# Matmul operands of 16 to 48 rows zero-filled to 128 rows, and two logit matmuls made one, in a hybrid decoder trunk

## The chip, the cores and the metric

The kernel runs on one core of one Trainium2 chip. The metric is the device time of one execution, in microseconds (us), as the median of several runs; lower is better. The engines are named as the profile names them: PE (TensorE, matmuls), PEld (its weight loads), DVE (VectorE), ACT (ScalarE), POOL (GpSimd), SP (SyncE, which only issues DMAs). A DMA that an engine issues is shown with a q behind the engine's name (ACTq).

## What is computed

One layer of a decoder trunk over 16 meta tokens and 512 tokens, model width 2048, all in float32. One input projection feeds three token mixers, and one output projection follows with a residual add and a final norm. Cut to the lines that matter here:

```python
N_META, CHUNK, BLOCK = 16, 64, 128
proj = rms_norm(x, norm_w) @ w_in              # one product for all mixers
(dq, dk, dv, dz, db, da, gq, gk, gv, gz, gl, fq, fk, fv, fz, ff) = split_cols(proj)

# A) gated DeltaNet, 6 heads x 128, chunks of 64
log_a = -exp(a_log) * softplus(da + dt_bias)   # a gate per head and token
g = cumsum(log_a)                              # per chunk
o_dn = gated_delta_rule_chunked(q_dn, k_dn, v_dn, log_a, sigmoid(db))

# B) GLA, 5 heads, key width 64, value width 128, chunks of 64
log_g = log_sigmoid(gl @ w_gk2 + b_gk) / 16    # gl: 16 columns (low rank), w_gk2: 16 x 320
o_gla = gla_chunked(gq, gk, gv, log_g)         # S_t = diag(exp log_g) S_{t-1} + k_t v_t^T

# C) forgetting attention, 5 heads x 128, blocks of 128 queries
c = cumsum(log_sigmoid(ff + b_f))
logits = q_i @ k.T + c_i[:, None] - c[None, :] # masked causally, softmax, times v

o = concat([o_dn, o_gla, o_fox])               # each normed and gated
out = rms_norm(x + o @ w_out)[:, 16:]          # meta tokens are dropped
```

The 16 meta tokens come first in the sequence, so each mixer has, beside four blocks of 128 tokens, a short block of 16.

## The kernel before

**Products and tiles.** Float32 operands of the projections are split into a high and a low part (fp32r), and a product is three matmuls: high by high, high by low, low by high (`inproj_part`, L245; `inproj_pair` and its `product`, L580, for the later columns; `mms`, L1410, for the output projection). A half of an input projection has 1024 weight columns per partition, loaded by `load_half`; `split` casts them on ACT (`whi`, L170) and subtracts on DVE (`wlo`, L171). It is 48 matmuls: 8 slices of the model width, three products, two parts of 264 tokens. Two halves are in flight. These projection matmuls fill PE; the mixers' small matmuls stand between them. A plain float32 matmul (not split) shows in the profile as two passes, a transpose as one.

**Order.** The kernel is written with a tile framework whose scheduler simulates a timeline and from it sets the order of every engine's instructions. A few places are tied by hand: `behind`, `later` and `place` pin a mixer's matmul behind a certain projection matmul, and `split` has priority. Any change to a cost or a dependence can therefore move instructions on all engines. On the chip each engine runs its list in order and waits at semaphores. A DMA is issued from an engine's list too, and a DMA that must wait for data holds up everything behind it on that engine.

**Pools.** Buffers are rings: `six` (14 large tiles: the gates' `gw` and `gcn`, attention operands), `t15` (6 tiles of 128 x 3 x 128: `dg`, `kdm`, `um`, `vpm`, `ym`, `gvm`, `gkm`), `row` (7), and in PSUM `psb` (4 banks, projections) and `psm` (4 banks, all the mixers' results).

**Places that the change touches**, in the order of time:

- *rstd diagonal* (L355 to L360). A matmul of `ones` with a diagonal matrix `dg` broadcasts the reciprocal norms along partitions, per block of 128 tokens; for the meta block (b = 4) both operands have 16 rows.
- *Gates* (`gates`, L456 to L474, and the lines ahead of it). `misc` holds the raw gate columns. `gw` has three rows of 528: `scm`, `gt` and `ga`, of which 17 partitions (32 to 48) are used; `ga` receives the running sum (`tensor_tensor_scan`, L466 on DVE). The sum is written to DRAM (`gd`, issued from ACT), read back as `gb`, spread over 128 partitions, and also transposed on PE (`ptg`, five transposes of 17 rows) into `gcol`. `gcn` (48 rows) holds the GLA low-rank gate `glr` and its weight `wgk`.
- *DeltaNet group g = 0, 1* (three heads each): `dn_keys` forms decays from `gb` and `gcol` (`at`, `e`) and the decayed meta keys `kdm`; `dn_inverse` gives `um`, 16 x 16 used; `dn_values` gives `vpm`; `dn_mix` multiplies `um` by `vpm` (`pym`, L853), copies that to `ym`, and forms the state after the meta tokens from `kdm` and `ym` (`ps0`, L858). All these operands have 16 rows.
- *GLA pair p = 0, 1, 2* (`gla_pair`; pair 2 has one head): `pgk` (L1001) is the low-rank gate, two matmuls of 48 rows; `gvm` and `gkm` are the meta values and keys, 16 rows, multiplied in `pg` (L1103; called pg0 here).
- *Forgetting attention* (`fox_head`): for each of four query blocks b, `pfa` (L1237) is the logits against all keys ahead of the block (16 + 128 b columns) and `pfd` (L1238) those against the block's own 128 keys, in two PSUM tiles.

Of the kernel before, what the change touches and what calls it, by code (L numbers as in the profile page):

```python
# [8 lines left out]
F32 = mybir.dt.float32  # L9
F32R = mybir.dt.float32r  # L10
# [4 lines left out]
ALU = mybir.AluOpType  # L15
# [3 lines left out]
P = 128  # L19
D = 2048  # L20
KT = D // P
NM = 16
S = 512
T = NM + S
HT = T // 2
NB = S // P
EPS = 1e-6
H = 3
# [54 lines left out]
def tile_hybrid_trunk(ctx, tc, xT, xtok, mtok, w_gate, w_in, w_out, w_dn, consts, lmask, fin_w, out, dbg=None):  # L83
# [271 lines left out]
    for b in range(5):  # L355
        r = NM if b == 4 else P
        dg = t15(f"dg{b}", (P, P))
        V.tensor_scalar_mul(dg[:r, :r], ident[:r, :r], rsc[:r, b : b + 1])
        o = pr[1][:, :NM] if b == 4 else pr[0][:, b * P : (b + 1) * P]
        PE.matmul(o, ones[:r], dg[:r, :r], start=True, stop=True)  # L360
    A.copy(rstd[:, NM:], pr[0])
# [85 lines left out]
    V.scalar_tensor_tensor(out=wgk, in0=whi.bitcast(F32), scalar=mcc[:48, 7:8], in1=raw, op0=ALU.mult, op1=ALU.add)  # L447
    A.copy(glr[0:32], misc[0:32])
# [7 lines left out]
    def gates():  # L456
        esc = cst.tile([P, 1], F32, name="esc")
        A.activation(esc[gr], mcc[gr, 2:3], AF.Exp)
        V.tensor_scalar(gt[gr], misc[gr], mcc[gr, 0:1], mcc[gr, 1:2], ALU.add, ALU.mult)
        V.scalar_tensor_tensor(out=ga[gr], in0=gt[gr], scalar=-1.0, in1=gt[gr], op0=ALU.mult, op1=ALU.min)  # L460
        A.activation(ga[gr], ga[gr], AF.Exp)
# [4 lines left out]
        V.tensor_tensor_scan(ga[gr], scm[gr], gt[gr], 0.0, ALU.mult, ALU.add)  # L466
        nc.scalar.dma_start(out=gd[:16], in_=ga[R0 : R0 + 16])
        nc.scalar.dma_start(out=gd[16:], in_=ga[R0 + 16 : R1])
        pt = psm.tile([P, 512], F32, tag="m", name="ptg")
        for b in range(NB):  # L470
            PE.transpose(pt[:, b * 17 : b * 17 + 17], ga[gr, NM + b * P : NM + (b + 1) * P], ident[gr, gr])
        PE.transpose(pt[:NM, 4 * 17 : 5 * 17], ga[gr, 0:NM], ident[gr, gr])
        V.tensor_copy(gcol[:, 0:4, :], pt[:, : 4 * 17].rearrange("p (b r) -> p b r", b=4))
        V.tensor_copy(gcol[:NM, 4, :], pt[:NM, 4 * 17 : 5 * 17])  # L474

# [160 lines left out]
    raw = {}  # L636
# [18 lines left out]
    def dn_keys(g):  # L655
# [25 lines left out]
        for b in (4, 0, 1, 2, 3):  # L681
# [16 lines left out]
            for j in range(H):  # L698
                dst = kd[:, b * H + j, :] if b < 4 else kdm[:, j, :]
                V.tensor_scalar_mul(dst, pk[:r, j * P : (j + 1) * P], e[:r, j, r - 1 : r])  # L700
# [34 lines left out]
    def dn_inverse(g, st):  # L735
# [31 lines left out]
        nc.scalar.dma_start(out=xm, in_=sc3.rearrange("h (a c) -> a h c", a=32))  # L767
        um = t15(f"um{g}", (32, H, 32))
        for o, x in ((um.rearrange("p h c -> p (h c)"), xm.rearrange("p h c -> p (h c)")),
                     (uc.rearrange("p n c -> p (n c)"), xc.rearrange("p n c -> p (n c)"))):  # L770
            waits.append((V.transpose(o, x).ins, len(splits) + SP[g], splits))
# [51 lines left out]
    def dn_values(g, st):  # L823
        vp = six.tile([P, NN, P], F32, tag="six", name=f"vp{g}")
        vpm = t15(f"vpm{g}", (NM, H, P))
        br = st["br"]
        for j in range(H):
            h = H * g + j
            v = row(f"v{h}")[:, :T]
            conv_silu(("dv", h), 12 + h, v)  # L830
            pv = psm.tile([P, 512], F32, tag="m", name=f"pv{h}")
            for b in range(NB):
                PE.transpose(pv[:, b * P : (b + 1) * P], v[:, bsl(b)], ident)
            for b in range(NB):
# [3 lines left out]
            V.tensor_scalar_mul(vpm[:, j, :], pv2[:NM, :P], br[:NM, 4, j : j + 1])  # L838
        st.update(vp=vp, vpm=vpm)
# [7 lines left out]
    def dn_mix(g, st):  # L847
# [4 lines left out]
        for j in range(H):  # L852
            PE.matmul(py[:NM, j * P : (j + 1) * P], st["um"][:NM, j, :NM], st["vpm"][:, j, :], start=True, stop=True)  # L853
        ym = t15(f"ym{g}")
        A.copy(ym[:NM], py[:NM, : H * P].rearrange("p (h d) -> p h d", h=H))
        p0 = psm.tile([P, 512], F32, tag="m", name=f"ps0{g}")
        for j in range(H):
            PE.matmul(p0[:, j * P : (j + 1) * P], st["kdm"][:, j, :], ym[:NM, j, :], start=True, stop=True)  # L858
        sst = t15(f"s0{g}")
# [115 lines left out]
    def gla_pair(p):  # L975
# [17 lines left out]
        x_sums(XSUM.get(p, ()))  # L993
        vm = t15(f"gvm{p}", (NM, 2, P))
        for e in range(ne):
            tok_values(inproj(("gv", 2 * p + e)), f"g{2 * p + e}", (vt3, qk)[e][:, 2], vt[:, e], vm[:, e])

        u, t = vt3[:R, 2], trow[:R, :T]
        for a in range(2):
            pg = psm.tile([P, 512], F32, tag="m", name=f"pgk{p}{a}")  # L1000
            PE.matmul(pg[:R, :HT], wgk[:, P * p : P * p + R], glr[:, a * HT : (a + 1) * HT],  # L1001
                      start=True, stop=True)
            V.tensor_scalar_add(u[:, a * HT : (a + 1) * HT], pg[:R, :HT], bgk[:R, p : p + 1])
# [164 lines left out]
    def fox_head(h):  # L1168
# [63 lines left out]
        for b in range(NB):  # L1232
            m = NM + b * P
            ts = bsl(b)
            pa = psm.tile([P, 512], F32, tag="m", name=f"pfa{h}{b}")
            pd = psm.tile([P, 512], F32, tag="m", name=f"pfd{h}{b}")
            PE.matmul(pa[:, :m], qT[:, ts], kT[:, :m], start=True, stop=True)  # L1237
            PE.matmul(pd[:, :P], qT[:, ts], kT[:, ts], start=True, stop=True)  # L1238
            pr = row(f"fp{h}{b}")[:, :T]
# [446 lines left out]
```

## Time and profile before

| | |
|---|---|
| time, median of 3 runs | 986.06 us (985.29 to 986.82) |
| span of the profiled execution | 986.9 us |
| PE busy | 974.9 us (99%), 7762 matmul passes |
| PEld busy | 893.7 us (91%) |
| DVE busy | 669.3 us (68%) |
| ACT busy | 480.3 us (49%) |
| POOL busy | 216.6 us (22%), 237 instructions |
| PE's share of the chain that ended last | 94% |
| DMA | 191.83 MB, mean 194 GB/s |

The profile gives no other time for its own execution than the span, which is 0.8 us above the median of the runs. A row of a timeline has the start, the busy length, engine, line, operation, output and inputs, the rows and columns of the array in use (PE), the shape, and how many instructions it stands for; lengths of neighbouring matmuls overlap, so what a matmul costs is read from one start to the next.

### The profile page before, as it was taken

Reading aid. Unit: us, or ns where it says so; the run is one execution under the profiler, and the core shown is the slowest. Engines: PE = TensorE matmul, PEld = TensorE weight load, DVE = VectorE, ACT = ScalarE, POOL = GpSimd, SP = SyncE. Lnnn points to the kernel's source line nnn. Section 1 sums busy time; section 2 is a strip of 40 time slices with the busy share of each in tenths; the row PEclk is TensorE's granted clock in tenths of the full one; section 3 lists DMA queues with packets and bytes.
Section 4 is the critical chain, followed back from the end, with each engine's and each line's share of the span. In section 5 each row is a group of like instructions: output and inputs, shape, how many; then the busy total and the mean of one; then the engine's idle time right before and its main releaser. Section 6 shows DMA issues by size and latency. Waiting matters only on the chain.

```text
span 986.9 us, 19830 instructions
## 1 busy us (share of the span) xinstructions
PE 974.9 (99%) x7762; PEld 893.7 (91%) x7762; DVE 669.3 (68%) x1462; ACT 480.3 (49%) x1051; POOL 216.6 (22%) x237
## 2 busy tenths in 40 slices
PE   9999999999999999999999999999999999999996
PEld 8899999899999888899899888899999998888885
DVE  5457786985657986334685756867767777887664
ACT  7654524344456344234446435655555544544354
POOL 0021322222123334201213121323322220000023
PEclk9999999999999999999999999999999999999999
DMA  9835588897458797644646556678766578456534
GB/s 348 296 122 206 162 237 237 233 260 223 128 164 221 209 255 198 157 107 102 158 134 164 145 143 197 186 208 226 205 198 164 191 238 295 162 193 211 193 128 172
DMA packets 70339, 191.83 MB, mean 194 GB/s; under 512 B 14077, under 2 KB 17325, under 8 KB 69476
## 3 DMA queue, kind: packets, MB, share of 16 engines
q1 hardware_dynamic: 46048, 152.53, 45.3%
q0 software_dynamic: 15104, 31.66, 18.2%
q10 hardware_dynamic: 9092, 6.36, 2.2%
q8 instruction: 61, 1.00, 0.4%
q14 instruction: 34, 0.28, 0.1%
HBM read 179.84 MB, written 60.88 MB: 244 GB/s over the span
## 4 chain that ended last, share of the span: by engine, by line
PE 94%; DMA 2%; DVE 1%; issue 1%; ACT 1%; POOL 0%; ACTq 0%; POOLq 0%; DVEq 0%
PE pp L245 46%; PE pp_a L580 8%; PE pq L1410 6%; PE pp L314 5%; PE pa L1410 3%; PE pt L1410 3%; PE ps L1410 3%; PE pp_b L580 2%; PE pp_d L580 2%; PE pp_c L580 2%; PE pr L1410 1%; PE pss L1059 1%; DMA zd<-gqk 1%; PE pgate L431 1%; PE pfo L1285 1%
## 5 line engine op out<-in xcount | busy, mean ns | idle before, releaser
L245 PE MATMUL pp<-xl,whi 128*128 128x264 f32 (+2 forms) x1120 | 273.7, 306 | 0.0
L245 PE MATMUL pp<-xh,whi 128*128 128x264 f32 (+2 forms) x1120 | 272.7, 306 | 0.0
L245 PE MATMUL pp<-xh,wlo 128*128 128x264 f32 (+2 forms) x1120 | 272.1, 305 | 0.0
L170 ACT CAST whi<-raw 128x1024 fp32r<-128x1024 f32 x131 | 137.3, 1048 | 185.1 <-PE pp L245 121.8
L171 DVE TENSOR_TENSOR wlo<-raw,whi 128x1024 fp32r<-128x1024 f32 x131 | 163.3, 1247 | 68.2 <-ACT whi L170 57.6
L245 PEld LDWEIGHTS pp<-xl,whi 128*128 128x128 f32 x1120 | 182.6, 189 | 9.2 <-issue 0.4
L245 PEld LDWEIGHTS pp<-xh,whi 128*128 128x128 f32 x1120 | 182.2, 188 | 9.3 <-issue 0.2
L245 PEld LDWEIGHTS pp<-xh,wlo 128*128 128x128 f32 x1120 | 182.6, 189 | 8.7 <-issue 0.2
L390 POOL TENSOR_SCALAR stc<-cv 128x528 f32<-128x528 f32 (+1 forms) x18 | 28.1, 1563 | 144.1 <-DVE cv L622 141.3
L622 DVE SCALAR_TENSOR_TENSOR cv<-pb,cpk,cv 128x528 f32<-128x528 f32 (+1 forms) x54 | 41.0, 760 | 0.8
L1439 POOL TENSOR_TENSOR acc<-acc,fw 128x512 f32<-128x512 f32 x4 | 6.1, 1537 | 138.6 <-DVE wll L171 138.6
L171 DVE TENSOR_TENSOR wlos<-raws,whis 128x1024 fp32r<-128x1024 f32 x20 | 24.2, 1221 | 15.0 <-ACT whis L170 15.0
L170 ACT CAST whis<-raws 128x1024 fp32r<-128x1024 f32 x20 | 20.7, 1049 | 27.9 <-PE ps L1410 9.4
L580 PE MATMUL pp_a<-t,whi 128*128 128x264 f32 (+1 forms) x224 | 30.3, 283 | 0.0
L580 PEld LDWEIGHTS pp_a<-t,whi 128*128 128x128 f32 x224 | 28.0, 188 | 0.4
L580 PE MATMUL pp_a<-xh,whi 128*128 128x264 f32 x112 | 28.1, 285 | 0.0
L580 PE MATMUL pp_a<-xl,whi 128*128 128x264 f32 x112 | 27.9, 285 | 0.0
L379 DVE TENSOR_TENSOR pb<-pp,rstd 128x264 f32<-128x264 f32 (+1 forms) x36 | 13.8, 422 | 18.9 <-PE pp L245 18.9
L1410 PE MATMUL pq<-whia,a 128*128 128x512 f32 x80 | 25.4, 393 | 0.0
L1410 PE MATMUL ps<-whis,s 128*128 128x512 f32 x80 | 25.4, 394 | 0.0
L1410 PE MATMUL pq<-whis,s 128*128 128x512 f32 x80 | 25.3, 394 | 0.0
L390 POOL TENSOR_SCALAR stdz<-zdz 128x512 f32<-128x512 f32 x6 | 11.2, 1875 | 63.3 <-DVE zdz L408 62.3
(506 smaller groups left out, 2106.4 us busy)
## 6 DMA issues: line engine op xcount, KB each, us to landing
raw<-in_w_in SPq DMA_DIRECT2D x103, 512.0 KB, 4.1
ti<-in_w_in SPq DMA_DIRECT2D x28, 512.0 KB, 5.3
raw<-ti SPq DMA_DIRECT2D x28, 512.0 KB, 4.3
tw<-in_w_dn SPq DMA_DIRECT2D x20, 512.0 KB, 5.1
raws<-tw SPq DMA_DIRECT2D x15, 512.0 KB, 4.2
ti<-in_w_in POOLq DMA_DIRECT2D x14, 512.0 KB, 6.4
ti<-ti POOLq DMA_DIRECT2D x14, 512.0 KB, 6.7
tw<-in_w_dn POOLq DMA_DIRECT2D x10, 512.0 KB, 7.0
```

The lines of the kernel that those rows point to most:

```text
L170: pace[0] = A.copy(hi, raw).ins
L171: pace[1] = V.tensor_tensor(out=lo, in0=raw, in1=hi.bitcast(F32), op=ALU.subtract).ins
L245: mm = PE.matmul(p_[:, :nt], wt[:, j * m : (j + 1) * m], xx[k][:, t0 : t0 + nt], start=(k == 0 and wt is hi and xx is xh), stop=(k == KT - ...
L314: mm = PE.matmul(ps[:, :S], wt[:, j * P : (j + 1) * P], xx[k][:, NM:T], start=(k == 0 and wt is hi and xx is xh), stop=(k == KT - 1 and wt ...
L379: V.tensor_tensor(out=o, in0=p_[rows], in1=rstd[rows, t0 : t0 + n], op=ALU.mult)
L390: maxes.append(G.tensor_scalar_max(t, src, LOW).ins)
L431: PE.matmul(pgate[a][:, :HT], wg[k // 8][:, k % 8, :], xx[k][:, a * HT : (a + 1) * HT], start=(k == 0 and xx is xh), stop=(k == KT - 1 and ...
L580: m = PE.matmul(p_[:, cols], wt[:, j * P : (j + 1) * P], xx[j][part_][:, cols], start=first and i == 0, stop=i == len(todo) - 1, skip_grou ...
L622: V.scalar_tensor_tensor(out=c, in0=pb[:, t0 + w : w + T], scalar=cwc[:, blk, w : w + 1], in1=c, op0=ALU.mult, op1=ALU.add)
L1059: mm = PE.matmul(ps[o0 : o0 + n, b * n : b * n + n], kx[rr, k0 : k0 + n], qx[rr, q0 : q0 + n], start=True, stop=True)
L1285: PE.matmul(po[:, qs], v_[:, js], p_[:, jb, qs], start=(jb + i == 0), stop=False)
L1410: mm = PE.matmul(p_, o_[:, s], w_, start=(first and n == 0), stop=(last and n == 2), skip_group_check=True)
```

## The change

Operands that had 16, 17 or 48 rows get 128 rows, the added ones zero, and the matmuls then use all 128 rows. The zeros come from POOL: a cast of a zero column over all of `gcn`, memsets of `ga` (ahead of the scan), `kdm`, `um`, `vpm`, `ym`, `gvm` and `gkm`. The rstd diagonal takes all rows of the identity, so it needs no fill. The gate transposes write 128 columns each into two PSUM tiles (`ptg`, `ptgm`), and the copies pick the 17 wanted. `pgk` of pair 2 gets 128 instead of 64 columns, `pym` 32 instead of 16 columns. In the attention, blocks 0 to 2 compute `pfa` and `pfd` as one matmul over 16 + 128 (b + 1) keys into one PSUM tile; block 3, whose 528 columns are more than the tile's 512, stays as it was. The projections are not touched. The core of the diff:

```diff
-        V.tensor_scalar_mul(dg[:r, :r], ident[:r, :r], rsc[:r, b : b + 1])
+        V.tensor_scalar_mul(dg[:, :r], ident[:, :r], rsc[:, b : b + 1])
-        PE.matmul(o, ones[:r], dg[:r, :r], start=True, stop=True)
+        PE.matmul(o, ones, dg[:, :r], start=True, stop=True)
...
-    gcn = six.tile([48, T + 320], F32R, tag="six", name="gcn")
+    gcn = six.tile([P, T + 384], F32R, tag="six", name="gcn")
+    G.tensor_copy(gcn, zero_c.to_broadcast([P, T + 384]))
...
+        G.memset(ga, 0.0)
         V.tensor_tensor_scan(ga[gr], scm[gr], gt[gr], 0.0, ALU.mult, ALU.add)
...
-            PE.transpose(pt[:, b * 17 : b * 17 + 17], ga[gr, NM + b * P : NM + (b + 1) * P], ident[gr, gr])
-        PE.transpose(pt[:NM, 4 * 17 : 5 * 17], ga[gr, 0:NM], ident[gr, gr])
+            PE.transpose(pt[:, b * P : (b + 1) * P], ga[:, NM + b * P : NM + (b + 1) * P], ident)
+        ptm = psm.tile([P, 512], F32, tag="m", name="ptgm")
+        PE.transpose(ptm[:NM, :P], ga[:, 0:NM], ident)
...
-        kdm = t15(f"kdm{g}", (NM, H, P))
+        kdm = t15(f"kdm{g}")
+        G.memset(kdm, 0.0)
...
-        um = t15(f"um{g}", (32, H, 32))
+        um = t15(f"um{g}", (P, H, 32))
+        G.memset(um, 0.0)
...
-        vpm = t15(f"vpm{g}", (NM, H, P))
+        vpm = t15(f"vpm{g}")
+        G.memset(vpm, 0.0)
...
-            PE.matmul(py[:NM, j * P : (j + 1) * P], st["um"][:NM, j, :NM], st["vpm"][:, j, :], start=True, stop=True)
+            PE.matmul(py[:32, j * P : (j + 1) * P], st["um"][:, j, :], st["vpm"][:, j, :], start=True, stop=True)
         ym = t15(f"ym{g}")
+        G.memset(ym, 0.0)
...
-            PE.matmul(p0[:, j * P : (j + 1) * P], st["kdm"][:, j, :], ym[:NM, j, :], start=True, stop=True)
+            PE.matmul(p0[:, j * P : (j + 1) * P], st["kdm"][:, j, :], ym[:, j, :], start=True, stop=True)
...
-        vm = t15(f"gvm{p}", (NM, 2, P))
+        vm = t15(f"gvm{p}", (P, 2, P))
+        G.memset(vm, 0.0)
...
-            PE.matmul(pg[:R, :HT], wgk[:, P * p : P * p + R], glr[:, a * HT : (a + 1) * HT],
+            PE.matmul(pg[:, :HT], wgk[:, P * p : P * p + P], glr[:, a * HT : (a + 1) * HT],
...
-        km = t15(f"gkm{p}", (NM, P))
-        A.copy(km[:, :R], pm[:NM, :R])
+        km = t15(f"gkm{p}", (P, P))
+        G.memset(km, 0.0)
+        A.copy(km[:NM, :R], pm[:NM, :R])
...
-            pd = psm.tile([P, 512], F32, tag="m", name=f"pfd{h}{b}")
-            PE.matmul(pa[:, :m], qT[:, ts], kT[:, :m], start=True, stop=True)
-            PE.matmul(pd[:, :P], qT[:, ts], kT[:, ts], start=True, stop=True)
+            if b < NB - 1:
+                pd = pa[:, m : m + P]
+                PE.matmul(pa[:, : m + P], qT[:, ts], kT[:, : m + P], start=True, stop=True)
+            else:
+                pd = psm.tile([P, 512], F32, tag="m", name=f"pfd{h}{b}")
+                PE.matmul(pa[:, :m], qT[:, ts], kT[:, :m], start=True, stop=True)
+                PE.matmul(pd[:, :P], qT[:, ts], kT[:, ts], start=True, stop=True)
```

**How the order moves.** Because the scheduler works from costs, the change moves instructions. The largest move is on DVE at the gates. Before, from the third gate step (L463) to the split of the next half; L379, L620 and L622 evacuate and convolve a projection result, L466 is the scan, which the listing shows by its general name:

```order
L379 TENSOR_TENSOR pb_687<-pp_0_689,rstd 128x264
L379 TENSOR_TENSOR pb_687<-pp_1_690,rstd 128x264
L620 TENSOR_SCALAR cv_803<-pb_687,cpk 128x528
L171 TENSOR_TENSOR wlo_1_877<-raw_1_873,whi_1_876 128x1024
L622 SCALAR_TENSOR_TENSOR cv_803<-pb_687,cpk,cv_803 128x528
L463 SCALAR_TENSOR_TENSOR gw<-gw 17x528
L622 SCALAR_TENSOR_TENSOR cv_803<-pb_687,cpk,cv_803 128x528
L464 TENSOR_SCALAR gw<-gw,esc,cpk 17x528
L622 SCALAR_TENSOR_TENSOR cv_803<-pb_687,cpk,cv_803 128x528
L466 SCALAR_TENSOR_TENSOR gw<-gw 17x528
L171 TENSOR_TENSOR wlo_0_949<-raw_0_945,whi_0_948 128x1024
```

Now (L464, L465 and L468 are the former L463, L464 and L466):

```order
L464 SCALAR_TENSOR_TENSOR gw<-gw 17x528
L465 TENSOR_SCALAR gw<-gw,esc,cpk 17x528
L468 SCALAR_TENSOR_TENSOR gw<-gw 17x528
L379 TENSOR_TENSOR pb_690<-pp_0_692,rstd 128x264
L379 TENSOR_TENSOR pb_690<-pp_1_693,rstd 128x264
L171 TENSOR_TENSOR wlo_1_880<-raw_1_876,whi_1_879 128x1024
```

The scan stood behind the evacuation and the split `wlo_1`, and now stands ahead of both. Further down the same list, the split `wlo_0` of the next half (`wlo_0_949` above, `wlo_0_952` now) has got the decay subtractions ahead of it, which read `gb`, the gates that come back by DMA (`e`, L728, 15 instructions):

```order
L728 TENSOR_SCALAR e_1187<-gb_688,gcol 16x16 x3
L728 TENSOR_SCALAR e_1200<-gb_688,gcol 128x128 x3
L728 TENSOR_SCALAR e_1213<-gb_688,gcol 128x128 x3
L728 TENSOR_SCALAR e_1226<-gb_688,gcol 128x128 x3
L728 TENSOR_SCALAR e_1239<-gb_688,gcol 128x128 x3
L171 TENSOR_TENSOR wlo_0_952<-raw_0_948,whi_0_951 128x1024
```

Before, no instruction that reads `gb` stood ahead of that split; now 15 do. On PE, the gate transposes stood in the second half of a projection block (`whi_1`, `wlo_1`; slices `xl_392` and `xh_391`):

```order
L245 MATMUL pp_0_816<-xl_392,whi_1_876 128x264
L471 MATMUL ptg<-ident,gw 128x17 x4
L472 MATMUL ptg<-ident,gw 16x17
L245 MATMUL pp_1_817<-xl_392,whi_1_876 128x264
L245 MATMUL pp_0_816<-xh_391,wlo_1_877 128x264
```

and now stand in the first half (`whi_0`) of the same block, 53 projection matmuls earlier:

```order
L245 MATMUL pp_0_819<-xl_156,whi_0_824 128x264
L245 MATMUL pp_1_820<-xl_156,whi_0_824 128x264
L473 MATMUL ptg<-ident,gw 128x128 x4
L475 MATMUL ptgm<-ident,gw 16x128
L245 MATMUL pp_0_819<-xh_155,wlo_0_825 128x264
```

In the attention, PE's list around head 0, block 0 had two logit matmuls with a transpose of the gate path (`pgt`) between them:

```order
L1144 MATMUL pgt_7136<-ident,gqk_6619 128x128
L1237 MATMUL pfa_7784<-fqk_7144 128x16
L1144 MATMUL pgt_7136<-ident,gqk_6619 128x128
L1238 MATMUL pfd_7785<-fqk_7144 128x128
L1144 MATMUL pgt_7136<-ident,gqk_6619 128x128 x2
```

Now there is one, of 144 columns:

```order
L1153 MATMUL pgt_7153<-ident,gqk_6634 128x128
L1247 MATMUL pfa_7801<-fqk_7161 128x144
L1153 MATMUL pgt_7153<-ident,gqk_6634 128x128
L583 MATMUL pp_c<-xh_303,whi_3480_8078 128x264
L1153 MATMUL pgt_7153<-ident,gqk_6634 128x128
```

Elsewhere the mixers' matmuls stand at the same projection matmul as before, or a few (up to 41) away. On POOL, the fills stand where their tiles are first written; at the gates, `kdm`, `gcn`, a small `pb` fill and then `ga`, ahead of the next activation product (`stc`).

More of the change, by code (lines that the diff above doesn't have):

```diff
@@ L446, in tile_hybrid_trunk @@
     V.tensor_scalar_mul(raw, raw, mcc[:48, 6:7])
-    V.scalar_tensor_tensor(out=wgk, in0=whi.bitcast(F32), scalar=mcc[:48, 7:8], in1=raw, op0=ALU.mult, op1=ALU.add)
+    V.scalar_tensor_tensor(out=wgk[:48, :320], in0=whi.bitcast(F32), scalar=mcc[:48, 7:8], in1=raw, op0=ALU.mult, op1=ALU.add)
     A.copy(glr[0:32], misc[0:32])
@@ L470, in gates @@
         for b in range(NB):
-            PE.transpose(pt[:, b * 17 : b * 17 + 17], ga[gr, NM + b * P : NM + (b + 1) * P], ident[gr, gr])
-        PE.transpose(pt[:NM, 4 * 17 : 5 * 17], ga[gr, 0:NM], ident[gr, gr])
-        V.tensor_copy(gcol[:, 0:4, :], pt[:, : 4 * 17].rearrange("p (b r) -> p b r", b=4))
-        V.tensor_copy(gcol[:NM, 4, :], pt[:NM, 4 * 17 : 5 * 17])
+            PE.transpose(pt[:, b * P : (b + 1) * P], ga[:, NM + b * P : NM + (b + 1) * P], ident)
+        ptm = psm.tile([P, 512], F32, tag="m", name="ptgm")
+        PE.transpose(ptm[:NM, :P], ga[:, 0:NM], ident)
+        V.tensor_copy(gcol[:, 0:4, :], pt.rearrange("p (b r) -> p b r", b=4)[:, :, gr])
+        V.tensor_copy(gcol[:NM, 4, :], ptm[:NM, gr])
     gates()
@@ L698, in dn_keys @@
             for j in range(H):
-                dst = kd[:, b * H + j, :] if b < 4 else kdm[:, j, :]
+                dst = kd[:, b * H + j, :] if b < 4 else kdm[:NM, j, :]
                 V.tensor_scalar_mul(dst, pk[:r, j * P : (j + 1) * P], e[:r, j, r - 1 : r])
@@ L767, in dn_inverse @@
         nc.scalar.dma_start(out=xm, in_=sc3.rearrange("h (a c) -> a h c", a=32))
-        um = t15(f"um{g}", (32, H, 32))
-        for o, x in ((um.rearrange("p h c -> p (h c)"), xm.rearrange("p h c -> p (h c)")),
+        um = t15(f"um{g}", (P, H, 32))
+        G.memset(um, 0.0)
+        for o, x in ((um[:32].rearrange("p h c -> p (h c)"), xm.rearrange("p h c -> p (h c)")),
                      (uc.rearrange("p n c -> p (n c)"), xc.rearrange("p n c -> p (n c)"))):
@@ L837, in dn_values @@
             PE.transpose(pv2[:NM, :P], v[:, 0:NM], ident)
-            V.tensor_scalar_mul(vpm[:, j, :], pv2[:NM, :P], br[:NM, 4, j : j + 1])
+            V.tensor_scalar_mul(vpm[:NM, j, :], pv2[:NM, :P], br[:NM, 4, j : j + 1])
         st.update(vp=vp, vpm=vpm)
```

2 lines of the change are left out of this document (1 added, 1 removed).

## Prediction

> **What bounds the kernel now.** I read the page's shares first, then the chain that ended last, then PE's waits, and only then the PE timeline around each touched line. The span, the shares and the chain, from the page:
>
> ```profile
> span 986.9 us, 19830 instructions
> ...
> PE 974.9 (99%) x7762; PEld 893.7 (91%) x7762; DVE 669.3 (68%) x1462; ACT 480.3 (49%) x1051; POOL 216.6 (22%) x237
> PE 94%; DMA 2%; DVE 1%; issue 1%; ACT 1%; POOL 0%; ACTq 0%; POOLq 0%; DVEq 0%
> ```
>
> TensorE (PE) sets the end: it is 94% of the chain. A microsecond taken out of PE's stream is a microsecond of time, unless PE then waits for something that did not become earlier. PE's largest waits by releaser, and the ScalarE instruction behind the first:
>
> ```profile
> PE pss L1059 <- ACT kq L1068: 1.3, 1, 1.3
> PE pss L1059 <- issue: 0.8, 1, 0.8
> PE pss L1059 <- DVE kq L1045: 0.7, 1, 0.7
> 549.01 0.65 ACT L1005 ACTIVATE gt<-gt 128x528 f32<-128x528 f32 x1 [6.71 <-DMA zd<-gqk]
> ```
>
> Columns are total, times, longest; a timeline row has start, busy length, engine, line, operation, count and, in brackets, the idle time before it and its releaser. PE waits at three places of the GLA scores, 2.8 us in all. The two of pair 1 (0.7 and 1.3) hang on ACT, which stood behind a DMA for 6.71 us until 549.01. Savings upstream of that DMA move everything; savings between it and the scores only lengthen the wait.
>
> **What a matmul of few rows costs.** The two `pgk` matmuls (48 rows) of GLA pair 0 stand in a stream of full 264-column ones:
>
> ```profile
> 490.83 0.28 PE L245 MATMUL pp<-xh,whi 128*128 128x264 f32 x1
> 490.95 0.27 PE L970 MATMUL pwg<-ident,gqk 128*16 128x128 f32 x1
> 491.15 0.38 PE L1001 MATMUL pgk<-gcn 48*128 48x264 f32 x1
> 491.46 0.39 PE L245 MATMUL pp<-xh,whi 128*128 128x264 f32 x1
> 491.69 0.41 PE L245 MATMUL pp<-xl,whi 128*128 128x264 f32 x2
> 492.03 0.38 PE L1001 MATMUL pgk<-gcn 48*128 48x264 f32 x1
> 492.34 0.39 PE L245 MATMUL pp<-xh,wlo 128*128 128x264 f32 x1
> ```
>
> "48*128" is rows by columns of the array in use. Read the starts, not the lengths (they overlap). A full matmul gives way after 0.12 us (490.83 to 490.95). Around the second `pgk` three things are longer: the full one ahead of it 0.22 (491.69 to 492.03 holds two, 0.34), its own step 0.31 (492.03 to 492.34), and the next full one 0.23, as after the first `pgk` (491.46 to 491.69). At 0.12 each they would take 0.37; they take 0.76. So the switch to fewer rows and back costs 0.39 us, and the array is empty around it. The transpose at 490.95 uses 16 columns and shows none of this, so transposes are exempt.
>
> The Trainium skill, TensorE: Matmul & The Clock Gate, Step-by-step: what each phase is for, says that time goes with the column count and that the row count does not matter. By that rule padding the rows would be worth 0 and the sum would be the attention merges alone. This case's rows disagree: 0.31 us for 48 rows, 0.12 for 128.
>
> **The change part by part.**
>
> *`pgk`, pairs 0 and 1, 48 to 128 rows.* The second saves 0.39; the first, from 490.95 to 491.69, 0.74 where 0.38 would do (0.14 for the transpose, two matmuls at 0.12), saves 0.36. Two pairs: 1.50.
>
> *`pgk`, pair 2, 48x64 to 128x128.* In the output-side stream:
>
> ```profile
> 602.24 0.39 PE L245 MATMUL pp<-xh,wlo 128*128 128x512 f32 x1
> 602.55 0.33 PE L1001 MATMUL pgk<-gcn 48*64 48x264 f32 x1
> 602.82 0.50 PE L245 MATMUL pp<-xh,whi 128*128 128x512 f32 x1
> ```
>
> Ahead of it 0.31 instead of 0.23 for 512 columns, its own 0.27 instead of 0.12, and 0.10 behind: 0.33. The second one is followed by more narrow matmuls, so its exit stays: 0.05. Together 0.38.
>
> *`ps0` (meta rows into the state, twice), 16 to 128 rows.*
>
> ```profile
> 245.01 0.41 PE L245 MATMUL pp<-xh,wlo 128*128 128x264 f32 x2
> 245.34 0.93 PE L858 MATMUL ps<-ym,kdm 16*128 16x128 f32 x6
> 246.20 0.38 PE L888 MATMUL pa<-qT,kT 128*128 128x128 f32 x1
> ```
>
> Entry 0.33 against 0.24; six passes 0.86 against six at 0.11 (a full 128-column f32 pass, an estimate, just under the 0.12 of 264 columns), 0.20; exit 0.10. That is 0.39, twice 0.78. `pym`, ahead of it, still has only 32 columns, so it stays a narrow tile: I cost it at 0, with 0.3 each as the far end.
>
> *`pg0` (GLA meta state, three pairs), 16 to 128 rows, still 64 columns.*
>
> ```profile
> 525.00 0.43 PE L1103 MATMUL pg<-gvm,gkm 16*64 16x128 f32 x4
> 525.37 0.88 PE L1113 MATMUL pgn<-gvt,gpr 128*64 128x128 f32 x12
> 526.17 0.39 PE L245 MATMUL pp<-xh,whi 128*128 128x264 f32 x1
> ```
>
> Twelve 128x64 passes take 0.80, 0.067 each; four in that mode would take 0.27 instead of 0.37, and the switch inside the group goes: 0.14 each, 0.43 in all. Entry and exit remain, as 128x64 is itself narrow.
>
> *The rstd diagonal, last block, 16 to 128 rows.*
>
> ```profile
> 51.18 1.37 PE L360 MATMUL pr<-dg,ones 128*128 128x128 f32 x10
> 52.48 0.51 PE L431 MATMUL pgate<-xh,wg 128*128 128x264 f32 x2
> ```
>
> Ten passes in 1.30; eight full ones at 0.11 leave 0.42 for the two short ones, which as full ones take 0.22. With 0.10 for the exit: 0.29.
>
> *Gate transposes, 17 to 128 rows.*
>
> ```profile
> 81.40 0.42 PE L471 MATMUL ptg<-ident,gw 17*128 17x17 f32 x4
> 81.77 0.39 PE L245 MATMUL pp<-xl,whi 128*128 128x264 f32 x1
> ```
>
> The five 17-column transposes take only 0.37 (81.40 to 81.77); five of 128 columns at 0.11 take 0.55. Entry 0.10 and exit 0.10 saved as at `pgk`, 0.18 more spent: 0.
>
> *Attention logits.* Block 0 of head 0, then block 1:
>
> ```profile
> 690.85 0.29 PE L1237 MATMUL pfa<-fqk 128*128 128x16 f32 x2
> 690.99 0.62 PE L580 MATMUL pp_b<-xh,wlo 128*128 128x264 f32 x3
> 691.44 0.38 PE L1238 MATMUL pfd<-fqk 128*128 128x128 f32 x2
> 691.58 0.37 PE L580 MATMUL pp_b<-xh,wlo 128*128 128x264 f32 x1
> 697.60 0.41 PE L1237 MATMUL pfa<-fqk 128*128 128x144 f32 x2
> 697.85 0.38 PE L1238 MATMUL pfd<-fqk 128*128 128x128 f32 x2
> ```
>
> `pfa` of 16 columns costs 0.14 to the next start and 0.08 more in the three behind it (0.45 against 0.37), 0.22; `pfd` much the same, 0.23. One pass pair of 144 columns costs 0.25 (697.60 to 697.85): 0.20 saved. Blocks 1 and 2 stream the same number of columns as before and take the time of their columns: 0.01. Five heads: 1.05.
>
> PE saves 0.29 + 1.50 + 0.38 + 0.78 + 0.43 + 1.05 = 4.43 us.
>
> **What is given back.** *Old waits.* The whole of `pgk` of pair 1 (0.75) lies between that DMA and pair 1's scores, so the waits of 0.7 and 1.3 grow by it. For pair 0's 0.8 wait and the attention I take 0.25 and 0.2. Ends: 0, and 2.2 if all of both pairs' `pgk` and half the attention are eaten. I take 1.2, since pair 1's is the one whose chain I can follow in the rows.
>
> *The gates, where the order moves.*
>
> ```profile
> 71.00 0.64 ACT L461 ACTIVATE gw<-gw 17x528 f32<-17x528 f32 x1 [3.44 <-DVE gw L460]
> 78.37 1.25 DVE L466 TENSOR_TENSOR_SCAN gw<-gw 17x528 f32<-17x528 f32 x1
> 87.17 0.50 DVE L693 TENSOR_SCALAR atm<-gb,gcol 16x16 f32<-16x16 f32 x3 [0.16 <-DMA gb<-gd]
> 88.86 1.84 DVE L693 TENSOR_SCALAR at<-gb,gcol 128x128 f32<-128x128 f32 x9
> 84.91 0.41 PE L245 MATMUL pp<-xh,wlo 128*128 128x264 f32 x2
> L171 DVE TENSOR_TENSOR wlo<-raw,whi 128x1024 fp32r<-128x1024 f32 x131 | 163.3, 1247 | 68.2 <-ACT whi L170 57.6
> L1013 POOL MEMSET a<- x3: 343/624/1055, 486.3 to 586.5; 128x256 f32 x3
> ```
>
> The order puts the scan on VectorE (DVE) ahead of the evacuation of `pb` and a weight split, and `ptg` 53 matmuls earlier on PE. PE reaches it at about 81.40 - 53 x 0.122 - 0.29 = 74.6. The scan ended at 79.62. ScalarE (ACT) was idle for 3.44 us until 71.00, waiting for DVE, so it is free at 67.56; the new order hands it its input by then. From there I count three ACT steps of 0.65 (this one, a cast to `gcn`, the logarithm), a DVE step of 0.7, the new memset of `ga` on GpSimd (POOL), which has to come between the last reader of `ga` and the scan, 0.7 (a 128x256 memset takes 0.34 to 1.06), and the scan, 1.25: 72.2, and with five changes of engine at 0.14, an estimate, 72.9. That leaves 1.7 us of slack, and PE does not wait for the transposes. But 15 subtractions from `gb` now stand ahead of the split `wlo_0` of the next half. `gb` came by DMA 7.5 us after the scan's end (87.1 against 79.62), so now at 80.4; the subtractions take 2.8 (by the rows at 87.17 and 88.86), the split 1.25 (the page's mean for L171): ready at 84.45. PE wants it at 84.91 - 0.29 = 84.6. I cost this at 0, with 0.15 of room; each microsecond that the scan is later than 72.9 costs nearly one. Far ends: nothing, and 5 us (below).
>
> *POOL and the rest.* Seventeen more POOL instructions, mostly memsets of 128x128 to 128x528; by the same row 0.3 to 1.1 each. POOL is 22% busy. Those in the GLA pairs stand ahead of DMAs that POOL issues, and pair 1's chain goes through such a transfer: I take 0.2, ends 0 and 0.7. The 15 PSUM tiles fewer only relax the ring; I cost that at 0.
>
> Sum: 4.43 - 1.2 - 0.2 = 3.0 us. The profiled execution, whose rows these are, has a span of 986.9 us, 0.8 above the median of the runs, 986.06; carried over, 986.06 - 3.0 = **983.0 us**.
>
> **Rivals.**
> 1. *All of it lands.* The old waits shrink with the rest, because the DMA behind them starts earlier too: 986.06 - 4.4 = 981.6. For it: the DMA's own issue may hang on PE further up. Against it: 549.01 shows ACT held by a DMA, and no PE work in between.
> 2. *Row count is not what drains.* Something else about these matmuls does (the new operand tile, or the f32 mode), and padding keeps the 0.3 us step: only the merges remain, 1.05 less 0.2: 985.2, no measurable change. For it: all the short matmuls also use other tiles. Against it: the transpose at 490.95 and the merge's neighbour at 697.60 change tiles and pass in 0.2 or less. The Trainium skill's rule quoted above would also give this.
> 3. *The `gb` wait takes it back.* The scan ends 2 us later than I worked out (POOL runs its memset late, behind `kdm`, `gcn` and `pb`, which now precede it), the split is ready at 86.4, PE waits 1.9: 984.9, within the bound of no change.
> 4. *Slower.* The scan does not come earlier at all: POOL's memset of `ga` or its wait holds it to its old end. PE then stands at `ptg` from 74.6 to 79.6, 5.0 us, and nothing behind makes it up, since PE has no slack anywhere: 986.06 - 3.0 + 5.0 = 988.1. It costs from a scan end of 74.6 on, and decides the sign at 77.6. For it: a cross-engine wait has been put into a chain PE now meets sooner. Against it: POOL is busy 22% of the time, and a lag of 6.7 us would need something in its queue that waits for a late engine.
>
> **How the numbers follow.** A measurement of this kernel can tell about 0.2% from no change, 1.97 us: faster is below 984.1, slower above 988.0. Forecast 0.56; all lands 0.12; no drain by rows 0.09; the `gb` wait 0.12; slower 0.06; a stall at a place that I have not seen, 0.05, split between the last two classes. Faster: 0.56 + 0.12, and a little of the `gb` case, 0.69. Same: 0.09 + most of 0.12 + 0.02, 0.22. Slower: 0.06 + 0.03, 0.09. The range goes from 981.0 (4.4, with 0.6 for `pym`) to 985.9, which takes in the second and third rival and leaves out the fourth. The forecast's own range is 982.2 to 983.8, from its two ends for the old waits.
>
> **What would show it.** In the profile after: steps of 0.12 around both `pgk`, with 128 rows; about 0.67 for the six passes of `ps0`; 0.27 for `pg0`; one `pfa` of 144 columns where `pfa` and `pfd` stood; PE's wait for pair 1's `kq` longer by some 0.75; a scan ending near 72.9 and `ptg` on PE near 74.6 with no idle time ahead of it; and no wait of PE for `wlo` near 84.6. The prediction is wrong if 128-row steps still take 0.3, or if a wait of over 1 us stands on PE between 74 and 90.

## The result, and the profile after

The changed kernel takes 988.53 us (median of 22 runs, 984.64 to 990.75), the kernel before 985.93 us (22 runs, 985.06 to 989.27): ratio 1.0022, 95% interval 1.0016 to 1.0027. Forecast was 983.0, faster. It is slower: by the ratio 2.2 us, just past the 0.2% that the prediction named. (Differences in us between kernels are worked out from such ratios here and below.)

From the page of the changed kernel, the span, the shares and the chain that ended last:

```profile
span 985.1 us, 19810 instructions
...
PE 971.6 (99%) x7732; PEld 891.3 (90%) x7732; DVE 670.4 (68%) x1462; ACT 479.3 (49%) x1051; POOL 229.6 (23%) x253
PE 90%; DMA 3%; DVE 2%; issue 2%; POOL 1%; ACT 1%; ACTq 0%; POOLq 0%; DVEq 0%
```

PE's busy time fell by 3.3 us, its share of the chain from 94% to 90%: more of the chain now runs through waits for other engines. This execution is not a typical one. Its time was 986.82 us, 1.7 below the kernel's median. A time is 1.7 us more than its span (986.82 and 985.1), so the profile of before, with a span of 986.9, was that of an execution of some 988.6 us (an estimate from these two numbers), 2.7 above *its* median. Both kernels were therefore profiled a second time. PE's waits in the first and in the second profile of the changed kernel (total, times, longest):

```profile
PE pp_a L583 <- ACT zfz L606: 1.6, 1, 1.6
...
PE pp L245 <- DVE wlo L171: 1.1, 3, 0.7
...
PE pss L1067 <- ACT kq L1076: 0.7, 1, 0.7
PE pp_a L583 <- ACT vf L597: 0.2, 1, 0.2
```

```profile
span 986.0 us, 19810 instructions
...
PE pp_a L583 <- ACT vf L597: 1.6, 1, 1.6
PE pp_a L583 <- ACT zfz L606: 1.6, 1, 1.6
...
PE pp L245 <- DVE wlo L171: 0.8, 3, 0.5
PE pss L1067 <- ACT kq L1076: 0.7, 1, 0.7
```

and in the second profile of before:

```profile
span 984.3 us, 19830 instructions
...
PE pss L1059 <- issue: 0.5, 1, 0.5
```

The 2.0 us at pair 1's scores (0.7 and 1.3), on which the prediction leaned, are not in this second execution. In the changed kernel new waits stand: two at `pp_a` (L583, the paired projections beside the attention) and three at `wlo`, between 341 and 355 us. The start of the same projection matmul in both second profiles, from the trace, shows where the time goes (the matmuls of the input projections, the gate columns among them, are counted in PE's order from 0):

| projection matmul number | before, us | after, us | after minus before |
|---|---|---|---|
| 2120 (ahead of the GLA gate blocks) | 340.21 | 339.53 | -0.7 |
| 2300 | 381.81 | 382.77 | +1.0 |
| 3200 (pair 1) | 548.14 | 547.16 | -1.0 |
| 3800 (attention, head 0) | 659.91 | 658.80 | -1.1 |
| 4300 | 733.92 | 734.29 | +0.4 |
| 4780 (end of the paired projections) | 803.92 | 806.31 | +2.4 |
| last matmul of PE | 976.16 | 977.92 | +1.8 |

PE loses 1.7 us between 2120 and 2300, where its three waits for `wlo` stand. It is ahead by 1.1 us when the attention starts and behind by 2.4 when the paired projections end.

**The steps that PE was to save are there.** Rows of the changed kernel's timeline (start, length, engine, line, output and inputs, array in use):

```profile
492.55 0.41 PE L245 MATMUL pp<-xh,wlo 128*128 128x264 f32 x2
492.79 0.28 PE L1009 MATMUL pgk<-gcn 128*128 128x264 f32 x1
492.91 0.41 PE L245 MATMUL pp<-xh,whi 128*128 128x264 f32 x2
...
245.16 0.83 PE L865 MATMUL ps<-ym,kdm 128*128 128x128 f32 x6
245.83 0.72 PE L895 MATMUL pa<-qT,kT 128*128 128x128 f32 x5
...
525.39 0.44 PE L1112 MATMUL pg<-gvm,gkm 128*64 128x128 f32 x4
525.66 0.83 PE L1122 MATMUL pgn<-gvt,gpr 128*64 128x128 f32 x12
...
51.01 1.18 PE L360 MATMUL pr<-dg,ones 128*128 128x128 f32 x10
52.04 0.49 PE L431 MATMUL pgate<-xh,wg 128*128 128x264 f32 x2
...
690.08 0.41 PE L1247 MATMUL pfa<-fqk 128*128 128x144 f32 x2
690.23 0.74 PE L583 MATMUL pp_a<-t,wlo 128*128 128x264 f32 x4
690.81 0.65 PE L583 MATMUL pp_d<-t,whi 128*128 128x264 f32 x4
```

`pgk` steps 0.12 with the one ahead of it and the one behind it plain too (0.31 before); `ps0` takes 0.67 (0.86), `pg0` 0.27 (0.37), the diagonal 1.03 (1.30). The merged `pfa` of block 0 costs 0.15 and 0.09 in the four behind it, 0.24 for 0.45.

Yet PE's busy time fell by no more than 3.0 to 3.3 us. It counts the slow steps behind a wait: in the second profile of the changed kernel, around the wait of 0.46 us that ends at 342.45, two steps (starts 341.61 to 342.79) take 1.18 us where two plain ones, of 0.23, take 0.46. So this wait costs 0.72, and the three for `wlo`, 0.8 as listed, cost the 1.7 of the table; the rest of it counts as busy.

### The profile page after: what moved, and what is told of

Its sections match the earlier page's. It is cut to its first block, busy times and chain, and to the rows that moved or that the text cites. A ratio compares the mean times of both kernels' runs of the same rounds, so it can differ in the third digit from the quotient of the medians.

```text
span 985.1 us, 19810 instructions
## 1 busy us (share of the span) xinstructions
PE 971.6 (99%) x7732; PEld 891.3 (90%) x7732; DVE 670.4 (68%) x1462; ACT 479.3 (49%) x1051; POOL 229.6 (23%) x253
## 4 chain that ended last, share of the span: by engine, by line
PE 90%; DMA 3%; DVE 2%; issue 2%; POOL 1%; ACT 1%; ACTq 0%; POOLq 0%; DVEq 0%
PE pp L245 43%; PE pp_a L583 7%; PE pq L1423 6%; PE pp L314 5%; PE pa L1423 3%; PE pt L1423 3%; PE ps L1423 3%; PE pp_b L583 2%; PE pp_d L583 2%; PE pp_c L583 2%; PE pr L1423 1%; DMA fqk<-gd 1%; PE pss L1067 1%; PE pgate L431 1%; PE pfo L1298 1%
## 5 line engine op out<-in xcount | busy, mean ns | idle before, releaser
L583 PE MATMUL pp_a<-t,whi 128*128 128x264 f32 (+1 forms) x224 | 30.8, 285 | 1.8 <-ACT zfz L606 1.6
L583 PEld LDWEIGHTS pp_a<-t,whi 128*128 128x128 f32 x224 | 28.2, 188 | 2.8 <-ACT zfz L606 1.8
L583 PE MATMUL pp_a<-xh,whi 128*128 128x264 f32 x112 | 28.2, 286 | 0.0
L583 PE MATMUL pp_a<-xl,whi 128*128 128x264 f32 x112 | 28.1, 286 | 0.0
L497 POOL DMA_DIRECT2D tw<-tw x16 | 13.4, 836 | 56.1 <-DVE wlo L171 35.3
L379 DVE TENSOR_TENSOR pb<-pp,rstd 128x264 f32<-128x264 f32 (+1 forms) x36 | 13.7, 423 | 18.4 <-PE pp L245 18.3
L170 ACT CAST whia<-rawa 128x1024 fp32r<-128x1024 f32 x15 | 15.5, 1048 | 20.4 <-PE pq L1423 7.0
```

The source lines that it names most:

```text
L170: pace[0] = A.copy(hi, raw).ins
L379: V.tensor_tensor(out=o, in0=p_[rows], in1=rstd[rows, t0 : t0 + n], op=ALU.mult)
L497: x = G.dma_start(out=out_[s], in_=in_[s], accum_op=ALU.add, max_dma_last_dim=2048)
L583: m = PE.matmul(p_[:, cols], wt[:, j * P : (j + 1) * P], xx[j][part_][:, cols], start=first and i == 0, stop=i == len(todo) - 1, skip_grou ...
```

## Experiments

Two theories. *Order*: PE's work shrinks as computed, but the schedule that the change brings makes PE wait elsewhere. *Cost*: the fills, or the merged tile, cost time of their own. All ratios are to the kernel before, run beside each kernel; in brackets the 95% interval.

**1. Second profiles.** Both kernels unaltered.

> The kernel before unaltered, for a second profile. If the 2.1 us of PE waits at pair 1's scores in its first profile (span 986.9, 2.7 us above what its median time gives) are not typical: a span near 984.2 us without most of them. If they are typical: the same waits within 0.3 us.

> The changed kernel unaltered, for a second profile. If its typical time holds waits that the first profile (986.8 us, faster than its median of 988.5) did not show: a span of 986 to 988 us and PE waits that add up to 1.5 to 2 us more than in the first. If the two profiles differ by noise spread evenly: the same waits, all a little longer.

Measured: 986.02 and a span of 984.3 for before; the changed kernel 1.0017 [1.0007, 1.0027], span 986.0. For before the first expectation held: the wait at pair 1's scores varies from one execution to the next. It was 2.0 us and nothing in the two profiles of this kernel, and of the five profiles below whose order ahead of the attention is that of before, four have it (1.5 to 2.0 us). For the changed kernel the span held (986.0), the waits did not: they add up to about 1 us more than in the first profile, not 1.5 to 2, though the second `pp_a` wait went from 0.2 to 1.6.

**2. Merge or rows.** `fox_only` has the last part of the diff alone, `rows_only` all but the last part.

> Only the three merged logit matmuls per head; every operand keeps its rows. If the loss comes from the attention (a wait of PE for ACT's zfz copy, which stands behind POOL's select and a DMA): 1.5 to 3 us slower than before, with such a wait near 702 us. If it comes from the row fills: 0.5 to 1 us faster than before, the 1.05 us of PE work less a little.

> All row fills, the attention as before. If the loss comes from the attention's new order: 1 to 2.5 us faster than before, with short waits for wlo between 340 and 355 us. If it comes from the fills and the order they cause: 2 to 4 us slower than before.

Measured: 1.0027 [1.0015, 1.0038] and 0.9995 [0.9983, 1.0008]. The merges alone lose as much as the whole change does; the fills gain less than expected.

**3. Places or tile.** The merges put the attention's transposes `pfx` (and all that follows them) behind later projection matmuls: head 0's blocks 1, 2, 3 at numbers 3853, 3921, 3996 where they had been at 3846, 3904, 3970, and those of heads 1 to 3 by 9 to 40 later. Merging block 0 alone leaves them where they were. So one kernel has the later places without a merge, the other a merge without them:

```diff
+    LATER = {'pfx01': 3853, 'pfx02': 3921, 'pfx03': 3996}
...
+        if tile in LATER:
+            later.append((mm.ins, LATER[tile] - 257))
```

> The kernel before, with no fill and no merge; only the probability transposes of head 0's blocks 1 to 3 are held back until the projection matmuls behind which the changed kernel has them (7, 17 and 26 later), and the rest of the attention follows to the changed kernel's places. If the later places cost the time: 2.5 to 4 us slower than before, with waits of PE at L580 near 702 and 740 us. If the merged tile itself costs it: within 0.7 us of before.

```diff
-            if b < NB - 1:
+            if b == 0:
```

> Only query block 0 of each head merged (one matmul of 144 columns); the attention then stands where it stood before. If the order was the loss: 0.7 to 1.2 us faster than before (five times 0.20) and no wait of PE at 702. If merging is the loss: 0.5 to 1.5 us slower, in proportion to the blocks merged.

Measured: 1.0019 [1.0010, 1.0028] with the places alone, 0.9997 [0.9988, 1.0005] with the merge alone. Later places cost 1.9 us with the matmuls of before. The kernel with the places alone has one wait of PE in the attention (beside 1.5 us at pair 1's scores),

```profile
PE pp_a L584 <- ACT vf L598: 1.6, 1, 1.6
```

which is the second of the two. The first, at 702, is missing there; the next experiment shows why. The gain of `merge_b0` (0.3 us, expected 0.7 to 1.2) is too small to tell from none; in its profile PE needs 335.3 us from projection matmul 3660 to its end, and 336.5 in the second profile of before, 1.2 less, so the 1.0 us of work is gone there.

**4. What the later places meet.** The chain in the second profile of the changed kernel, in order of time: ACT issues the DMA that brings the next head's gate row, POOL's mask select (L1234) waits for it, POOL's next work is the activation product `stfz`, ACT waits for that, and behind it on ACT stand the exponential of the current block and the copy `zfz` that frees PE's bank:

```profile
693.17 0.33 ACTq L1230 DMA_DIRECT2D fqk<-gd  x1
699.63 0.82 POOL L1234 TENSOR_SCALAR_AFFINE_SELECT fqk<-fqk 128x128 f32<-128x128 f32 x1 [6.42 <-DMA fqk<-gd]
700.45 1.48 POOL L390 TENSOR_SCALAR stfz<-zfz 128x512 f32<-128x512 f32 x1
701.96 0.63 ACT L391 ACTIVATE stfz<-stfz 128x512 f32<-128x512 f32 x1 [2.92 <-POOL stfz L390]
703.00 0.35 ACT L606 COPY zfz<-pp_a 128x264 f32<-128x264 f32 x1
703.41 1.87 PE L583 MATMUL pp_a<-t,whi 128*128 128x248 f32 x14 [1.58 <-ACT zfz L606]
```

The same in the second profile of before:

```profile
691.20 0.33 ACTq L1221 DMA_DIRECT2D fqk<-gd  x1
696.11 0.29 POOL L1225 TENSOR_SCALAR_AFFINE_SELECT fqk<-fqk 128x128 f32<-128x128 f32 x1 [4.79 <-DVE fsm L1246]
696.39 1.48 POOL L390 TENSOR_SCALAR stfz<-zfz 128x512 f32<-128x512 f32 x1
697.91 0.63 ACT L391 ACTIVATE stfz<-stfz 128x512 f32<-128x512 f32 x1
700.73 0.36 ACT L603 COPY zfz<-pp_a 128x264 f32<-128x264 f32 x1
```

The place in POOL's queue is not new: in before too the select stands ahead of the product, and the DMA landed at 695.96, all but together with the DVE result that the row names (696.02). What is new is that no time to spare is left behind it. In before the bank was free at 701.1 and PE came to the same place in its list at 704.2: 3.1 us to spare. In the changed kernel the DMA is issued 2.0 us later and takes 6.3 us to land, not 4.8 (why it takes longer is not shown); the bank is free at 703.4, and PE, with fewer of the attention's matmuls ahead of this place, wants it at 701.8. The wait at 740 has the same chain: the select stands 5.53 us for the DMA, until 737.23, with the product behind it.

The kernel with the places alone agrees. On its POOL the product stands ahead of the select at the first place, where PE does not wait:

```profile
699.87 2.31 POOL L394 TENSOR_SCALAR stfz<-zfz 128x512 f32<-128x512 f32 x1 [2.63 <-PE pfx L1259]
704.02 1.17 POOL L1229 TENSOR_SCALAR_AFFINE_SELECT fqk<-fqk 128x128 f32<-128x128 f32 x1 [1.84 <-DMA fqk<-gd]
```

At the second, where PE waits, the select stands ahead: it starts at 739.34, after 5.25 us of standing for the DMA, and the product at 739.77. To test this, the select alone is ordered behind the activation product, for the later heads (PE's order is that of `fox_only`, matmul for matmul):

```diff
+            x = G.affine_select(out=o, in_=i, ...)
+            if h > H1:
+                tc.add_manual_dep(x.ins, maxes[-1].name, mybir.DependencyInfo(
+                    mybir.DependencyClass.NoSync, mybir.DependencyReason.DATA), reason="behind")
```

> The three merges per head alone, as in the run fox_only, with one thing more: POOL's mask select of the next head, which waits for a DMA, is ordered behind the activation product stfz instead of ahead of it. PE's order stays that of fox_only. If the wait of 1.7 us at 702 comes from that place in POOL's queue: it is gone or under 0.5, the wait near 740 stays, and the time lies 0.8 to 2 us under fox_only's 1.0027, at 1.0005 to 1.002 of before. If it comes from PE's later places alone: the wait stays.

Measured: 0.9997 [0.9988, 1.0006], 3.0 us under `fox_only`. Both `pp_a` waits are gone, the second one too, which was expected to stay, and the merges now give what was worked out: from projection matmul 3660 to its end PE needs 335.4 us, 1.1 less than in the second profile of before (`fox_only`: 339.3). In this kernel's trace POOL no longer waits for the DMA there:

```profile
698.66 2.31 POOL L390 TENSOR_SCALAR stfz<-zfz 128x512 f32<-128x512 f32 x1 [2.76 <-PE pfx L1262]
700.94 0.28 POOL L1225 TENSOR_SCALAR_AFFINE_SELECT fqk<-fqk 128x128 f32<-128x128 f32 x1
701.56 0.63 ACT L391 ACTIVATE stfz<-stfz 128x512 f32<-128x512 f32 x1
702.60 0.36 ACT L603 COPY zfz<-pp_a 128x264 f32<-128x264 f32 x1
```

So the attention's loss is POOL's select, standing for a DMA ahead of work that PE needs, once the later places had used up the 3.1 us to spare.

**5. Which fills cost.** Only the fills of `kdm`, `um`, `vpm`, `ym`; then each half; then the GLA part alone (`gcn`, `gvm`, `gkm`, `pgk`, `pg0`). Each is the corresponding parts of the diff and nothing else.

> Only the DeltaNet fills (kdm, um, vpm, ym), which by themselves bring the changed order around 320 to 360 us. If that order takes back what the rows save: 0 to 0.8 us slower than before, with PE waits for wlo of 0.3 to 0.9 near 342, 348 and 355 us. If the waits come from other fills: 0.6 to 0.9 us faster.

> Of the DeltaNet part only kdm and ym filled and ps0 with 128 rows: the build already shows that this alone brings the changed order between 320 and 360 us. If the order costs it: 1.5 to 3 us slower than before, with the wlo waits at 342, 348 and 354 us, though PE's work is 0.8 us less. If the number of fills costs it: half of what all four fills cost (1.0028), 1 to 1.5 us.

> The other half, um and vpm filled and pym with 128 rows: as many POOL memsets as the run kdm_ym_fill, but the order stays that of before. If order is what costs: within 0.7 us of before, no waits at 342 to 355 us. If POOL's fills cost it: 1 to 1.5 us slower.

> Only the GLA part: gcn, gvm and gkm filled, pgk and pg0 with 128 rows, order nearly that of before. PE's work is 1.50 + 0.38 + 0.43 = 2.3 us less; with 0.75 eaten by pair 1's scores 1.0 to 2.0 us faster. If a row-padded matmul gives nothing in the end: within 0.5 us of before.

Measured: 1.0028 [1.0018, 1.0038]; 1.0026 [1.0018, 1.0035]; 1.0005 [0.9996, 1.0014]; 0.9976 [0.9966, 0.9987]. As many POOL memsets, as long in all (1.7 and 1.9 us in the traces), cost 2.6 us where the order moves and 0.5 or nothing where it does not, so POOL's fills themselves are not what costs. The GLA part, whose order stays but for the gate transposes, gives 2.4 us for 2.3 us of PE work. `deltanet_only` was expected at 0 to 0.8 us and cost 2.8, and the mechanism that I had named for its order is only part of it. That mechanism: in the changed kernel DVE reaches the triangular solve (`ab`, which waits for a DMA) before it has split the next weights; before, the split came first. First the second profile of the changed kernel, then that of before:

```profile
338.71 0.20 DVE L760 TENSOR_TENSOR ab<-ab 51x30 f32<-51x30 f32 x1 [4.69 <-DMA ab<-scr]
...
341.19 1.21 DVE L171 TENSOR_TENSOR wlo<-raw,whi 128x1024 fp32r<-128x1024 f32 x1
```

```profile
337.00 1.23 DVE L171 TENSOR_TENSOR wlo<-raw,whi 128x1024 fp32r<-128x1024 f32 x1
...
338.52 0.20 DVE L756 TENSOR_TENSOR ab<-ab 51x30 f32<-51x30 f32 x1 [0.30 <-DMA ab<-scr]
```

`deltanet_only` has waits of PE for `wlo` from this, and larger ones in the GLA scores:

```profile
PE pss L1063 <- issue: 1.8, 2, 1.1
...
PE pp L245 <- DVE wlo L171: 0.8, 4, 0.3
```

`kdm_ym_fill`, with the same places on PE, has none for `wlo` between 340 and 356 us, against its expectation. DVE has the same order there, and the split ended at 343.31, but PE, late from a wait at the first weights, came to it only at 344.23. Its waits:

```profile
PE pss L1061 <- issue: 1.8, 3, 0.8
PE pp L314 <- ACT w2q L170: 1.5, 1, 1.5
```

Both kernels share two waits at later scores of pair 1, ending near 566 and 576 us (1.35 us together in `kdm_ym_fill`, 1.79 in `deltanet_only`), which no other profile here has; the profile names nothing that ends them. What this half costs over all its runs is thus measured (2.6 us) and tied to the order by its counterpart, but the cause of these shared waits stays open.

**6. The order kept.** All fills but DeltaNet's, and the merge of block 0 only; PE's places are those of before except the gate transposes and shifts by one or two matmuls.

> All fills but DeltaNet's, and the merge of block 0 alone: everything whose order on PE stays as before but for the gate transposes and two GLA places. If order is the whole loss: 0.29 + 1.50 + 0.38 + 0.43 + 1.0 = 3.6 us of PE work less 0.8 to 1.2 eaten by pair 1's scores, so 2.2 to 3.0 us faster than before. If fills cost time of their own (POOL, or DVE beside it): less than 1.5 us faster.

Measured: 983.70 us, 0.9982 [0.9974, 0.9991]: 1.8 us faster, a little under the expected 2.2 to 3.0, though its interval (0.9 to 2.6 us) reaches into that.

**7. Inside the changed kernel.** The select behind; without the `kdm` and `ym` fills; both.

> The changed kernel whole, with only POOL's mask select of the next head ordered behind the activation product. If that queue place is the attention's whole loss inside the changed kernel too: the waits at 702 and 739 are gone and it is 2 to 3.5 us faster than the changed kernel, 1 to 2 us faster than before (0.998 to 0.999). If the fills add losses there: still no faster than before.

> The changed kernel without the fills of kdm and ym (ps0 keeps 16 rows), which alone had moved the DeltaNet part. If that order costs 1.9 us net, as the step from gla_fills to rows_only says: 1.5 to 2.5 us faster than the changed kernel, within 0.8 us of before, with PE steps back to normal between 340 and 356 us and the attention's waits still there. If kdm's loss belongs to runs without GLA fills only: as slow as the changed kernel.

> Both at once: no kdm and ym fill, select behind. If the two order changes are the whole loss: 3 to 4 us faster than before (0.996 to 0.997), PE work 3.65 us less and only pair 1's wait left. If something else holds it back: 1.5 us or less.

Measured: 0.9985 [0.9976, 0.9993]; 1.0013 [1.0001, 1.0024]; 0.9984 [0.9974, 0.9994]. One line of order on POOL turns the changed kernel from 2.2 us slower to 1.5 us faster. `after_no_kdm` missed its 1.5 to 2.5 us: it is 0.4 to 0.9 faster than the changed kernel, which the intervals do not tell from nothing. Beside the select, taking out the DeltaNet fills adds nothing: their order, which cost 2.6 us alone, costs here about as much as the 0.8 us that `ps0` saves. `after_both` missed its 3 to 4 us. PE's waits in it, but for one at the start that all kernels have:

```profile
PE pfx L1269 <- DVE fm L1264: 0.7, 1, 0.7
PE pss L1065 <- issue: 0.6, 1, 0.6
PE pss L1065 <- ACT kq L1074: 0.6, 1, 0.6
PE pa L1424 <- ACT whio L170: 0.4, 1, 0.4
```

Against the second profile of before (0.5 in all) 1.8 us more: of the 3.65 us of PE work (as forecast, without `ps0`) 1.85 are left, and the spans differ by 1.7 (982.6 and 984.3). The prediction had put such losses at 1.2, but at pair 1's scores above all; here 0.6 of it stands there, 0.7 in the attention and 0.4 at the output projection.

The fastest is `gla_fills` (984.28 us, 0.9976), faster than both kernels; `kept_order` and the two with the select behind cannot be told from it by their intervals.

## Why the prediction was wrong

- *PE saves 4.43 us*: right in its terms. The steps came out as worked out from the rows, and between the same projection matmuls the stretches with `ps0`, `pgk`, `pg0` and the merges shorten to within 0.1 us of the forecast where no new wait stands (for the merges, in `select_behind`). The gate transposes, put at 0, cost 0.2 (matmuls 300 to 600). Busy time shows only 3.0 to 3.3 of it, as said above.
- *Few rows are what costs* (rival 2, that something else does, had 0.09): right. The Trainium skill, TensorEngine Tiling (Array Packing), Key Properties, says that a change of tiling mode drains TensorE; the trace agrees, 0.39 us per excursion of `pgk`, gone at 128 rows. The sentence on the row count that the prediction takes from the Trainium skill is written there of the weight load, and the weight loads of `pgk` agree with it: 0.18 us for 48 rows in the first profile of before, 0.19 for 128 in that of the changed kernel. It is the matmul's step that differs.
- *The gates*: right, closely. The scan ended at 72.7 (72.9 forecast), `ptg` stood at 74.34 with no wait ahead of it (74.6), the `wlo_0` split was done at 83.3 (84.45), in time. One term had no row beside it, 0.14 us for a change of engine; where the count starts in the profile of before, ACT followed DVE by 0.03 (70.97 to 71.00).

```profile
71.45 1.25 DVE L468 TENSOR_TENSOR_SCAN gw<-gw 17x528 f32<-17x528 f32 x1
74.34 0.60 PE L473 MATMUL ptg<-ident,gw 128*128 128x128 f32 x4
82.08 1.21 DVE L171 TENSOR_TENSOR wlo<-raw,whi 128x1024 fp32r<-128x1024 f32 x1
```

- *What failed: the places in the attention were given no price.* The order had the attention's transposes 7 to 40 projection matmuls later. The prediction has no term for this; of the attention's side effects it names only the 15 PSUM tiles fewer, a ring relaxed, at 0. A mixer's matmul that comes later on PE delays the mixer's chain (DVE, ACT's DMA issue, POOL, ACT), whose end PE needs at an unchanged place, and PE comes there sooner. The 3.1 us that this chain had to spare were gone after the move: two waits of up to 1.6 us, 3.0 us of time by `select_behind`. The prediction followed only what comes earlier.
- *A second miss: the DeltaNet order.* DVE's wait for the solve's DMA moved ahead of a weight split, which the prediction does not have; it costs 1.7 us between matmuls 2120 and 2300, of which `ps0`, elsewhere, gives back 0.8.
- *Old waits eat 1.2*: the size is near what `after_both` has (1.8), but by luck, as most of that stands elsewhere, and the base was not sound. The 2.0 us of waits at pair 1 in the profile of before stand in some executions and not in others. They did not grow by 0.75 either: in all eight profiles with the GLA fills PE waits there for ACT, 0.3 to 1.0 us. I also set span against median as if they were one measure; with 1.7 us between span and time, the profile was 2.7 us off the median, not 0.8.
- The chance for a stall at an unseen place was 0.05. With an order of all engines remade by a scheduler it should have been several times that. Rival 4 names nearly the measured time (988.1), by a late scan that did not happen: that it is near is chance.

## What to carry to other kernels

When a scheduler orders the engines, a change of operand shapes is a change of order, and both must be priced: compare the places of the small matmuls in the main stream in both directions, and for one that comes later, follow its chain through every in-order queue to the next wait of the main engine. Look in particular for an instruction that waits for a DMA standing ahead of one that the main engine needs; one order dependence there was worth 3.0 us here, of 4.4 us that all the matmuls were to save. And keep a small matmul at the full 128 rows and columns when it stands in a stream of full ones, as long as the fill leaves the order as it was: 2.4 us from six `pgk` and ten `pg0` passes.

## What the hardware showed beyond that

- The same DMA (`fqk`, 264 KB, once per head) took from 3.1 to 6.8 us to land within one execution of before (second profile), and from 3.1 to 6.7 in the changed kernel.
- POOL's activation product of 128x512 took 1.48 us in one run and 2.31 in another (`stfz`, at 700.45 and 698.66 above), at the same place of two programs.
- PE's wait at pair 1's scores was 2.0 us in one execution and 0 in another of the same program; one profile is one draw of it.
- A wait of PE costs more than its length: the one of 0.46 us listed at 342.45 cost 0.72, by the starts around it.
